# The first loads and transposes by halves, and the last chunks of the last half by quarters, in a two-layer encoder trunk

## The chip, the cores and the metric

The kernel runs on one NeuronCore of one Trainium2 chip, alone. The metric is the device time of one execution in microseconds, from start to end. It is given as the median of several executions.

## The reference, cut to what matters

Two layers of a post-norm encoder trunk over 256 tokens of width 1024: SwiGLU, a mixer, SwiGLU, each followed by a layer norm of the scaled residual. Layer 0 has a bidirectional mLSTM as its mixer, layer 1 a windowed attention. All data are float32.

```
D_MODEL = 1024; SEQ = 256; DEPTH = 2; D_FF = 2816; ALPHA = (2 * DEPTH) ** 0.25

def layer_norm(x, g, b):
    mu = mean(x, -1);  var = mean((x - mu) ** 2, -1)
    return (x - mu) * rsqrt(var + 1e-5) * g + b

def swiglu(x, w_in, w_out):
    gu = x @ w_in
    g, u = gu[..., :D_FF], gu[..., D_FF:]
    return (silu(g) * u) @ w_out

for l in range(DEPTH):
    x = layer_norm(ALPHA * x + 0.5 * swiglu(x, ffn_w_in[l, 0], ffn_w_out[l, 0]), ln_g[l, 0], ln_b[l, 0])
    x = layer_norm(ALPHA * x + mixer(x), ln_g[l, 1], ln_b[l, 1])     # mLSTM in layer 0, attention in layer 1
    x = layer_norm(ALPHA * x + 0.5 * swiglu(x, ffn_w_in[l, 1], ffn_w_out[l, 1]), ln_g[l, 2], ln_b[l, 2])
```

## The kernel before

**Split operands.** Every float32 operand of a product is held as two float32r tiles, a high part (a rounded copy, made by ScalarE for weights) and a low part (the difference, made by VectorE). One product is three matmuls: high by high, high by low, low by high (`mm3`). Nearly all matmuls have a 128x128 stationary operand and 512 columns of the moving one. In the profile the products with the input weights write banks named pw (`wbank`, four buffers), and the products with the output weights write banks named py (`ybank`, four buffers). The two pools share the eight banks of PSUM.

**Weights.** The class `Weights` holds a plan, a list of pieces of 128x1024 float32 in the order of their use. `load` starts the transfer of a piece on SyncE's queue (SP) as soon as a raw buffer is free; there are `RAW_BUFS = 4` buffers named w_raw for these. `high` makes w_hi on ScalarE, and `low` makes w_lo on VectorE and then gives the raw buffer back, so that `load` can start the next transfer. Piece 0 alone is split in two steps of 512 columns (the `if i == 0`). Which of these steps stands where in the engines' instruction streams is set by a model of the engines' times (`Paced`) during the feed-forward stages.

**The input.** x lies as two tiles of 128 tokens (x_69 and x_70 in the listings below, t = 0 and 1 in the code). Each is loaded in two halves of 512 columns on ScalarE's queue, between the first weight loads on SP: x0's first half, piece 0, x1's first half, piece 1, x0's second half, x1's second half, then the other pieces. `to_xT` transposes four blocks of 128x128 of one half on TensorE into a bank of its own and splits them into xT_hi and xT_lo. These banks are kept (`turned`), because four sums and differences of the transposed halves (S1 to S4) are made from them later.

**The start.** `ffn` is called first with `pending` of None. It puts out 14 transposes of the identity that nobody reads (`warm`), transposes the first half of x0, splits piece 0, and puts out 8 more idle transposes. `first_mm` then takes the products of pieces 0 and 1 in an order written out by hand: with a = 0 (piece 0, which holds the rows k = 0 and 1 of the reduction) the two products of high by high for x0, the transposes of x1's first half, then the other products of x0 and those of x1; with a = 1 first the transposes of both second halves.

**The end.** `tail` finishes a stage. For the last one it has six chunks c of the hidden layer left, for two token tiles t and two halves o of the output columns: y[t][o] is a bank of 128x512. Tile 0 goes first, both halves; each half is then added to the residual and its statistics are taken (`Norm.half`), and `Norm.finish` applies the layer norm. Tile 1 goes in the order half 1 with chunks 0 to 2, half 0 with all six, half 1 with chunks 3 to 5. After that VectorE does the last half, and `finish(1)`: aggregate the statistics, 1/sqrt by a power on GpSimd, subtract the mean and multiply by g in two halves, multiply by 1/sqrt and add b in two halves, and after each of the latter a DMA of that half of the result on SP. With `last`, `cuts` holds the two halves.

All instructions of the wrapped engines carry line 138 in the profile, since a helper records them.

Of the kernel before, what the change touches and what calls it, by code (L numbers as in the profile page):

```python
# [146 lines left out]
class Weights:  # L147
# [66 lines left out]
    def high(self):  # L214

        nc, i = self.nc, self.made
        p = self.plan[i]
        while self.half and (p["word"] not in self.raw or any(h[0] == p["needs"] for h in self.half)):
            self.low()
        while any(s_[0] == p["needs"] or p["word"] not in self.raw for s_ in self.sums):  # L220
            self.sum()
        if p["word"] not in self.raw:
            return False
        scale, raw = p["scale"], self.raw[p["word"]]
        hi = self.pool.tile([128, D], FR, name="w_hi", tag="w_hi", bufs=RING)
        if i == 0:
            for j in range(2):
                s_ = slice(j * 512, j * 512 + 512)
                nc.scalar.copy(hi[:, s_], raw[:, s_])
        elif scale is None:  # L230
            nc.scalar.copy(hi, raw)
        else:
            nc.scalar.activation(hi, raw, AF.Copy, scale=scale())
        self.half.append((i, hi))
        self.made += 1
        return True

    def low(self):

        nc = self.nc  # L240
        i, hi = self.half.pop(0)
        p = self.plan[i]
        k, scale, raw = p["k"], p["scale"], self.raw[p["word"]]
        lo = self.pool.tile([128, D], FR, name="w_lo", tag="w_lo", bufs=RING)
        if i == 0:
            for j in range(2):
                s_ = slice(j * 512, j * 512 + 512)
                nc.vector.tensor_sub(lo[:, s_], raw[:, s_], hi[:, s_].bitcast(F32))
        elif scale is None:
            nc.vector.tensor_sub(lo, raw, hi.bitcast(F32))  # L250
        else:
            nc.vector.scalar_tensor_tensor(lo, raw, scale(), hi.bitcast(F32), op0=OP.mult, op1=OP.subtract)
        self.parts[i] = (hi.rearrange("p (k f) -> p k f", k=k), lo.rearrange("p (k f) -> p k f", k=k))
        self.sums += [(i, *sum_) for sum_ in self.after.get(i, ())]
        self.drop(p["word"])
        self.load()
# [64 lines left out]
def trunk_kernel(ctx: ExitStack, tc: tile.TileContext, x, ffn_w_in, ffn_w_out, ln_g, ln_b, ml_w_in, ml_gate_b,  # L321
# [28 lines left out]
    def wide(w, r0, c0):  # L350
        piece(two(w, r0, c0), 2)
# [37 lines left out]
    for j, (kind, l, i, _) in enumerate(stages):  # L389
        if kind == "ffn":  # L390
            wi, wo = ffn_w_in[l, i], ffn_w_out[l, i]
            nth = iter(range(2 * UNITS))

            def down(n):
                for _ in range(n):
                    rows(wo, next(nth))

            for c0 in (0, F):
                for a in range(4):
                    wide(wi, a * 256, c0)  # L400
            for g in range(GROUPS):
                c0 = 512 + 768 * g
                for a in range(4):
                    beside(wi, a * 256, c0, F + c0)
                down(2)
                seven(wi, c0 + 256, F + c0 + 256, lambda i_: down(1) if g < GROUPS - 1 or i_ < 2 else None)
            down(6)
        elif kind == "mlstm":
            for c0 in (1024, 1536):
                for a in range(4):  # L410
                    wide(ml_w_in[0], a * 256, c0)
            for c0 in range(0, 1024, 256):
                for a in range(2):
                    narrow(ml_w_in[0], a * 512, c0)
            for c0 in (2048, 2560):
                for a in range(4):
                    wide(ml_w_in[0], a * 256, c0)
            for c in range(8):
                rows(ml_w_out[0], c, (lambda c=c: gcol[:, c:c + 1]))
        else:  # L420
            for c0 in (1024, 0):
                for a in range(4):
                    wide(at_w_in[0], a * 256, c0)
            for c0 in (512, 768):
                for a in range(2):
                    narrow(at_w_in[0], a * 512, c0)
            for c in range(8):
                rows(at_w_out[0], c)
        ends[j] = len(words)
# [98 lines left out]
    class Norm:  # L528
        def __init__(self, t, ca, eps, gb, last=False):
            self.t, self.ca, self.eps, self.gb, self.last = t, ca, eps, gb, last  # L530
            self.stats = state.tile([128, 2, 6], F32, name="stats", tag="stats", bufs=2)

        def half(self, h, y):
            z = xt[self.t][:, h * 512:(h + 1) * 512]
            nc.vector.scalar_tensor_tensor(z, z, self.ca, y, op0=OP.mult, op1=OP.add)
            nc.vector.bn_stats(self.stats[:, h], z)

        def finish(self, spare):
            mv = state.tile([128, 2], F32, name="mv", tag="mv", bufs=2)
            nc.vector.bn_aggr(mv, self.stats)  # L540
            rs = state.tile([128, 2], F32, name="rs", tag="rs", bufs=2)
            nc.vector.tensor_scalar(rs[:, 0:1], mv[:, 1:2], self.eps, None, op0=OP.add)
            nc.gpsimd.tensor_tensor(rs[:, 1:2], rs[:, 0:1], mhalf[:, 0:1], op=OP.pow)
            z = xt[self.t]
            cuts = [slice(0, 512), slice(512, D)] if self.last or self.t and LC[bound[0]] else [A]
            for s_ in cuts:
                nc.vector.scalar_tensor_tensor(z[:, s_], z[:, s_], mv[:, 0:1], self.gb[0][:, s_],
                                               op0=OP.subtract, op1=OP.mult)
            if len(cuts) == 1:
                W.done(0, spare)  # L550
            for s_ in cuts:
                nc.vector.scalar_tensor_tensor(z[:, s_], z[:, s_], rs[:, 1:2], self.gb[1][:, s_],
                                               op0=OP.mult, op1=OP.add)
                if self.last:
                    nc.sync.dma_start(out[0, tok(self.t), s_], z[:, s_])
            if len(cuts) > 1:
                W.done(0, spare)

    def tail(y, h, todo, first, norm, last, turn_at, between=None):

        def one(t, o, n):
            c, (i, w) = todo[t][n]
            mm3(y[t][o], h(c, t), pair(w, A, 0, slice(o * 512, o * 512 + 512)), first and n == 0, n == len(todo[t]) - 1)

        for o in range(2):
            for n in range(len(todo[0])):
                if between is not None and o == 1 and n == turn_at:
                    between()
                one(0, o, n)
            norm[0].half(o, y[0][o])  # L570
        norm[0].finish(0)
        full = len(todo[1])
        half = full // 2
        order = [(1, n) for n in range(half)] + [(0, n) for n in range(full)] + [(1, n) for n in range(half, full)]
        more = iter(RS[8 * bound[0]:8 * bound[0] + 8])
        for j, (o, n) in enumerate(order):
            if j == full + turn_at:
                emit_x(0, last)
            one(1, o, n)
            if j >= half and (n < half) == (o == 0):  # L580
                W.done(todo[1][n][1][0] + 1, next(more))
            if n == full - 1:
                norm[1].half(o, y[1][o])
        norm[1].finish(1)
        W.done(most=TD[bound[0]])
        return lambda: emit_x(1, last)
# [5 lines left out]
    def ffn(l, i, n, pending, last):  # L592
        with ExitStack() as ph:
# [10 lines left out]
            start = pending is None  # L604
            if start:
                warm(14)
                to_xT(0, xt[0], ybank, (0,), nc.vector.tensor_copy)
                W.split(1)
                warm(8)
            hs, pieces = [], []  # L610

            def tr(hB, t, h):
# [15 lines left out]

            def first_mm(ps, a):

                def mm(t, i, j):
                    for k in (2 * a, 2 * a + 1):
                        nc.tensor.matmul(ps[t], xT[i][:, k, tok(t)], pieces[a][j][:, k % 2], start=i == j == k == 0,
                                         stop=False)

                if a == 1:
                    for t in range(2):
                        to_xT(t, xt[t], ybank, (1,))
                pieces.extend(W.take(1))
                mm(0, 0, 0)  # L640
                if a == 0:
                    to_xT(1, xt[1], ybank, (0,))
                    W.split(2)
                mm(0, 1, 0)
                if a == 0:
                    mm(0, 0, 1)
                mm(1, 0, 0)
                if a == 0:
                    mm(1, 0, 1)
                mm(1, 1, 0)  # L650
                if a == 1:
                    mm(0, 0, 1)
                    mm(1, 0, 1)
# [757 lines left out]
```

## Time and profile before

| what | value |
|---|---|
| median of 3 executions | 930.31 us (929.8 to 930.38) |
| the profiled execution | 929.11 us |
| its span, from the first to the last instruction | 927.4 us |
| outside the span | 1.7 us |
| TensorE matmuls busy | 916.2 us (99% of the span) |
| VectorE busy | 784.6 us (85%) |
| ScalarE busy | 543.9 us (59%) |

The profile is of one execution. Times in it are microseconds from the first instruction. PE is TensorE, PEld its weight loads, DVE is VectorE, ACT is ScalarE, POOL is GpSimd, SP is SyncE; a q behind an engine's name is its queue, from which DMAs are issued. In the timeline a row gives start, duration, engine, line, operation, result and operands, form, and the number of like instructions; in brackets stands how long the engine had been idle before it, and what ended that. In the chain of waits a row gives start, duration and what the time was spent on. The granted clock of TensorE is a share of its full speed.

### The profile page before, as it was taken

What the parts mean: (1) busy time and instruction counts of PE and PEld (TensorE: products, weight loads), DVE (VectorE), ACT (ScalarE), POOL (GpSimd) and SP (SyncE); (2) the same over time, 40 slices, a digit from 0 to 9 for tenths busy, and PEclk for the clock granted to TensorE, in tenths of its full rate; (3) what the DMA queues carried; (4) which work ended last, traced back from release to release, by engine and by line L of the source; (5) the groups of instructions that cost most, each with busy time, mean ns of one, the idle gap of its engine ahead of it and who ended that gap; (6) DMA issues with size and microseconds to landing.
All of it is one profiled execution on the core that took longest, in us unless ns stands there. A gap on an engine that the chain in (4) does not pass through costs nothing.

```text
span 927.4 us, 12512 instructions
## 1 busy us (share of the span) xinstructions
PE 916.2 (99%) x4506; PEld 766.4 (83%) x4506; DVE 784.6 (85%) x948; ACT 543.9 (59%) x766; POOL 99.8 (11%) x144
## 2 busy tenths in 40 slices
PE   9999999999999999999999999999999999999996
PEld 7788888889988888888888888888888888888885
DVE  5899997886699799988887998978868878998875
ACT  5656756347564548565646666564568555757460
POOL 0010103011111010101010101010435300110100
PEclk9999999999999999999999999999999999999999
DMA  8979773646536949685558697737434385969421
GB/s 283 351 179 323 207 267 74 229 132 191 197 109 209 333 105 343 168 300 136 167 182 309 170 321 211 252 69 226 147 132 132 95 275 198 274 192 347 122 86 45
DMA packets 98461, 187.54 MB, mean 202 GB/s; under 512 B 6720, under 2 KB 37456, under 8 KB 98400
## 3 DMA queue, kind: packets, MB, share of 16 engines
q1 hardware_dynamic: 91072, 173.04, 54.4%
q0 software_dynamic: 6752, 12.66, 8.6%
q10 hardware_dynamic: 576, 1.05, 0.3%
q8 instruction: 35, 0.57, 0.2%
q14 instruction: 26, 0.21, 0.1%
HBM read 185.68 MB, written 1.05 MB: 201 GB/s over the span
## 4 chain that ended last, share of the span: by engine, by line
PE 91%; DVE 5%; ACT 2%; issue 1%; POOL 1%; DMA 0%; DVEq 0%; ACTq 0%; POOLq 0%
PE pw L138 58%; PE py L138 33%; DVE w_lo L138 2%; DVE h L138 1%; DMA w_raw<-in_ffn_w_in_dram 0%; ACT w_hi L138 0%; DVE wt L138 0%; POOL sc L1272 0%; DVE sc L138 0%; DVE a_lo L138 0%; DVE hst L138 0%; ACT S_hi L138 0%; DVE pr_lo L138 0%; ACT h L138 0%; DVE x L138 0%
## 5 line engine op out<-in xcount | busy, mean ns | idle before, releaser
L138 DVE TENSOR_TENSOR w_lo<-w_raw,w_hi 128x1024 fp32r<-128x1024 f32 (+1 forms) x237 | 281.8, 1219 | 25.9 <-ACT w_hi L138 23.8
L138 ACT CAST w_hi<-w_raw 128x1024 fp32r<-128x1024 f32 (+1 forms) x237 | 241.1, 1048 | 80.7 <-PE py L138 24.1
L138 PE MATMUL pw<-w_hi,xT_hi 128*128 128x512 f32 x560 | 221.8, 397 | 0.0
L138 PE MATMUL pw<-w_lo,xT_hi 128*128 128x512 f32 x560 | 217.5, 390 | 0.5 <-DVE w_lo L138 0.5
L138 PE MATMUL pw<-w_hi,xT_lo 128*128 128x512 f32 x560 | 218.0, 390 | 0.0
L138 ACT CAST w_hi<-s_raw 128x1024 fp32r<-128x1024 f32 x144 | 148.1, 1052 | 76.6 <-DVE s_raw L138 41.6
L138 DVE TENSOR_TENSOR w_lo<-s_raw,w_hi 128x1024 fp32r<-128x1024 f32 x144 | 172.8, 1219 | 21.2 <-ACT w_hi L138 20.5
L138 PE MATMUL py<-w_hi,h_hi 128*128 128x512 f32 x352 | 138.0, 392 | 0.0
L138 PE MATMUL py<-w_lo,h_hi 128*128 128x512 f32 x352 | 137.1, 390 | 0.0
L138 PE MATMUL py<-w_hi,h_lo 128*128 128x512 f32 x352 | 137.1, 389 | 0.0
L138 PEld LDWEIGHTS pw<-w_lo,xT_hi 128*128 128x128 f32 x560 | 105.3, 188 | 22.0 <-DVE w_lo L138 1.6
L138 PEld LDWEIGHTS pw<-w_hi,xT_lo 128*128 128x128 f32 x560 | 105.0, 188 | 22.4
L138 PEld LDWEIGHTS pw<-w_hi,xT_hi 128*128 128x128 f32 x560 | 105.1, 188 | 20.5 <-ACT w_hi L138 0.5
L138 DVE TENSOR_TENSOR s_raw<-s_raw 128x1024 f32<-128x1024 f32 x72 | 87.1, 1220 | 1.0
L267 POOL DMA_DIRECT2D s_raw<-in_ffn_w_in_dram x24 | 29.2, 1215 | 509.3 <-DVE w_lo L138 468.3
L138 PEld LDWEIGHTS py<-w_hi,h_lo 128*128 128x128 f32 x352 | 66.1, 188 | 13.9
L138 PEld LDWEIGHTS py<-w_lo,h_hi 128*128 128x128 f32 x352 | 66.1, 188 | 13.7 <-DVE w_lo L138 0.3
L138 PEld LDWEIGHTS py<-w_hi,h_hi 128*128 128x128 f32 x352 | 66.1, 188 | 13.4
L138 PE MATMUL pw<-w_hi,S_hi 128*128 128x512 f32 x192 | 74.7, 389 | 0.0
L138 PE MATMUL pw<-w_lo,S_hi 128*128 128x512 f32 x192 | 74.7, 389 | 0.0
L138 PE MATMUL pw<-w_hi,S_lo 128*128 128x512 f32 x192 | 74.7, 389 | 0.0
L138 DVE TENSOR_TENSOR h_lo<-pw,h_hi 128x512 fp32r<-128x512 f32 x44 | 30.1, 687 | 26.7 <-ACT h_hi L138 26.6
(206 smaller groups left out, 1087.2 us busy)
## 6 DMA issues: line engine op xcount, KB each, us to landing
w_raw<-in_ffn_w_out_dram SPq DMA_DIRECT2D x88, 512.0 KB, 5.1
s_raw<-in_ffn_w_in_dram SPq DMA_DIRECT2D x72, 512.0 KB, 6.1
w_raw<-in_ffn_w_in_dram SPq DMA_DIRECT2D x56, 512.0 KB, 5.1
w_raw<-in_ffn_w_in_dram SPq DMA_DIRECT2D x96, 256.0 KB, 4.3
s_raw<-in_ffn_w_in_dram POOLq DMA_DIRECT2D x24, 512.0 KB, 6.1
w_raw<-in_ml_w_in_dram SPq DMA_DIRECT2D x24, 512.0 KB, 4.6
w_raw<-in_at_w_in_dram SPq DMA_DIRECT2D x12, 512.0 KB, 4.2
w_raw<-in_ml_w_out_dram SPq DMA_DIRECT2D x8, 512.0 KB, 3.7
```

The costliest lines, as they stand in the source:

```text
L138: r = f(out, *args, **kw)
L267: nc.gpsimd.dma_start(t.rearrange("p (k f) -> p k f", k=self.words[w]["k"]), v, accum_op=OP.add)
```

## The change

Four edits, at the two ends of the program.

1. Piece 0 is loaded by two DMAs, one for each of its two blocks k of 512 columns, and piece 1 is split by halves as piece 0 is.
2. At the start the first two of the four transposes of x0's first half go to a bank of their own (`early`, a pw bank), and are split at once by VectorE alone. All four are then transposed again into the bank that is kept, of which the last two are split. The second group of idle transposes has 6 instead of 8.
3. In `first_mm` with a = 0, only the product with k = 0 stands ahead of the transposes of x1, and the product with k = 1 behind them.
4. At the end the accumulation of half 1 of tile 1 is closed after chunks 0 to 2 and added to the scaled residual (`first`). Chunks 3 to 5 go into two new pw banks of 128x256, one for each quarter; each quarter is added and its statistics are taken as it is done (`quarter`), so that there are three sets of statistics. The last scaling goes in pieces of 512, 256 and 256 columns, and the last of their three DMAs is issued from ScalarE's queue.

The diff:

```
 def high / def low:
-        if i == 0:
+        if i < 2:
             for j in range(2):
                 s_ = slice(j * 512, j * 512 + 512)
...
                 for a in range(4):
-                    wide(wi, a * 256, c0)
+                    if j == c0 == a == 0:
+                        piece([two(wi, 0, 0)[:, k:k + 1] for k in range(2)], 2)
+                    else:
+                        wide(wi, a * 256, c0)
...
     class Norm:
-            self.stats = state.tile([128, 2, 6], F32, name="stats", tag="stats", bufs=2)
+            self.stats = state.tile([128, 3, 6], F32, name="stats", tag="stats", bufs=2)
+            self.parts = 2
...
+        def first(self, h, y):
+
+            z = xt[self.t][:, h * 512:(h + 1) * 512]
+            nc.vector.scalar_tensor_tensor(z, z, self.ca, y, op0=OP.mult, op1=OP.add)
+
+        def quarter(self, h, q, y):
+            z = xt[self.t][:, h * 512 + q * 256:h * 512 + (q + 1) * 256]
+            nc.vector.tensor_add(z, z, y)
+            nc.vector.bn_stats(self.stats[:, h + q], z)
+            self.parts = 3
...
-            nc.vector.bn_aggr(mv, self.stats)
+            nc.vector.bn_aggr(mv, self.stats[:, 0:self.parts])
...
-            for s_ in cuts:
+            if self.parts == 3:
+                cuts = [slice(0, 512), slice(512, 768), slice(768, D)]
+            for n_, s_ in enumerate(cuts):
...
-                    nc.sync.dma_start(out[0, tok(self.t), s_], z[:, s_])
+                    (nc.scalar if n_ == 2 else nc.sync).dma_start(out[0, tok(self.t), s_], z[:, s_])
...
     def tail:
-            mm3(y[t][o], h(c, t), pair(w, A, 0, slice(o * 512, o * 512 + 512)), first and n == 0, n == len(todo[t]) - 1)
+            end = n == len(todo[t]) - 1 or last and t == o == 1 and n == len(todo[t]) // 2 - 1
+            mm3(y[t][o], h(c, t), pair(w, A, 0, slice(o * 512, o * 512 + 512)), first and n == 0, end)
...
+            if last and j == full + half:
+                break
             one(1, o, n)
+            if last and j == half - 1:
+                norm[1].first(1, y[1][1])
...
+        if last:
+            for q in range(2):
+                yq = wbank((128, 256))
+                for n in range(half, full):
+                    c, (i, w) = todo[1][n]
+                    mm3(yq, h(c, 1), pair(w, A, 0, slice(512 + 256 * q, 768 + 256 * q)), n == half, n == full - 1)
+                norm[1].quarter(1, q, yq)
...
     def ffn:
                 warm(14)
-                to_xT(0, xt[0], ybank, (0,), nc.vector.tensor_copy)
+                early = wbank((128, 2, 128))
+                for k in range(2):
+                    nc.tensor.transpose(early[:, k], xt[0][:, tok(k)], ident)
+                split_evac(pair(xT, A, slice(0, 2), tok(0)), early, high=nc.vector.tensor_copy)
+                late = ybank((128, 4, 128))
+                for k in range(4):
+                    nc.tensor.transpose(late[:, k], xt[0][:, tok(k)], ident)
+                turned[0, 0] = late
                 W.split(1)
-                warm(8)
+                split_evac(pair(xT, A, slice(2, 4), tok(0)), late[:, 2:4])
+                warm(6)
...
     def first_mm:
-                def mm(t, i, j):
-                    for k in (2 * a, 2 * a + 1):
+                def mm(t, i, j, ks=(2 * a, 2 * a + 1)):
+                    for k in ks:
...
-                mm(0, 0, 0)
                 if a == 0:
+                    mm(0, 0, 0, (0,))
                     to_xT(1, xt[1], ybank, (0,))
                     W.split(2)
-                mm(0, 1, 0)
+                    mm(0, 1, 0, (0,))
+                    mm(0, 0, 0, (1,))
+                    mm(0, 1, 0, (1,))
+                else:
+                    mm(0, 0, 0)
+                    mm(0, 1, 0)
```

What TensorE has in its stream at the start, before the change (x_69 and x_70 are the two token tiles, ident the identity; rows 1 and 3 are the idle transposes):

```order
1 L138 MATMUL py<-ident 128x128 x14
2 L138 MATMUL py<-ident,x_69 128x128 x4
3 L138 MATMUL py<-ident 128x128 x8
4 L138 MATMUL pw<-w_hi,xT_hi 128x512 x2
5 L138 MATMUL py<-ident,x_70 128x128 x4
6 L138 MATMUL pw<-w_hi,xT_lo 128x512 x2
7 L138 MATMUL pw<-w_lo,xT_hi 128x512 x2
8 L138 MATMUL pw<-w_hi,xT_hi 128x512 x2
9 L138 MATMUL pw<-w_lo,xT_hi 128x512 x2
10 L138 MATMUL pw<-w_hi,xT_lo 128x512 x2
11 L138 MATMUL py<-ident,x_69 128x128 x4
12 L138 MATMUL py<-ident,x_70 128x128 x4
```

And with the change, at the same place:

```order
1 L138 MATMUL py<-ident 128x128 x14
2 L138 MATMUL pw<-ident,x_69 128x128 x2
3 L138 MATMUL py<-ident,x_69 128x128 x4
4 L138 MATMUL py<-ident 128x128 x6
5 L138 MATMUL pw<-w_hi,xT_hi 128x512
6 L138 MATMUL py<-ident,x_70 128x128 x4
7 L138 MATMUL pw<-w_hi,xT_lo 128x512
8 L138 MATMUL pw<-w_hi,xT_hi 128x512
9 L138 MATMUL pw<-w_hi,xT_lo 128x512
10 L138 MATMUL pw<-w_lo,xT_hi 128x512 x2
11 L138 MATMUL pw<-w_hi,xT_hi 128x512 x2
12 L138 MATMUL pw<-w_lo,xT_hi 128x512 x2
```

The number of transposes ahead of the first product is 26 in both. One product of high by high has moved behind the transposes of x_70, so that ten matmuls stand between those and the next transposes before, and eleven now (rows 7 to 12 and two of w_hi by xT_lo).

VectorE's stream at the end of the program, from the last instructions of tile 0 (x_69) to the last of tile 1 (x_70), before:

```order
734 L138 SCALAR_TENSOR_TENSOR x_69<-x_69,rs,ln_b 128x512 x2
735 L138 SCALAR_TENSOR_TENSOR x_70<-x_70,py 128x512
736 L138 BN_STATS stats<-x_70 128x6
737 L138 SCALAR_TENSOR_TENSOR x_70<-x_70,py 128x512
738 L138 BN_STATS stats<-x_70 128x6
739 L138 BN_AGGR mv<-stats 128x2
740 L138 TENSOR_SCALAR rs<-mv 128x1
741 L138 SCALAR_TENSOR_TENSOR x_70<-x_70,mv,ln_g 128x512 x2
742 L138 SCALAR_TENSOR_TENSOR x_70<-x_70,rs,ln_b 128x512 x2
```

And now:

```order
735 L138 SCALAR_TENSOR_TENSOR x_69<-x_69,rs,ln_b 128x512 x2
736 L138 SCALAR_TENSOR_TENSOR x_70<-x_70,py 128x512 x2
737 L138 BN_STATS stats<-x_70 128x6
738 L138 TENSOR_TENSOR x_70<-x_70,pw 128x256
739 L138 BN_STATS stats<-x_70 128x6
740 L138 TENSOR_TENSOR x_70<-x_70,pw 128x256
741 L138 BN_STATS stats<-x_70 128x6
742 L138 BN_AGGR mv<-stats 128x2
743 L138 TENSOR_SCALAR rs<-mv 128x1
744 L138 SCALAR_TENSOR_TENSOR x_70<-x_70,mv,ln_g 128x512 x2
745 L138 SCALAR_TENSOR_TENSOR x_70<-x_70,rs,ln_b 128x512
746 L138 SCALAR_TENSOR_TENSOR x_70<-x_70,rs,ln_b 128x256 x2
```

The residual of the last half is now scaled ahead of the first half's (row 736 holds both), two pairs of an addition and its statistics over 256 columns stand where one pair over 512 stood, and the last scaling has three steps instead of two. Between the two places the streams of all engines hold the same instructions in the same order.

More of the change, by code (lines that the diff above doesn't have):

```diff
@@ L244, in low @@
         lo = self.pool.tile([128, D], FR, name="w_lo", tag="w_lo", bufs=RING)
-        if i == 0:
+        if i < 2:
             for j in range(2):
```

## The prediction

> **What bounds the kernel now.** First the page: the engines' busy times and the chain of work that ended last.
>
> ```profile
> PE 916.2 (99%) x4506; PEld 766.4 (83%) x4506; DVE 784.6 (85%) x948; ACT 543.9 (59%) x766; POOL 99.8 (11%) x144
> PE 91%; DVE 5%; ACT 2%; issue 1%; POOL 1%; DMA 0%; DVEq 0%; ACTq 0%; POOLq 0%
> ```
>
> TensorE (PE) holds 91% of the chain. The change leaves the middle of the program as it is, so only the pieces at the ends that aren't PE can go. Second, the chain of waits over the first 36 us, to see what the start hangs on:
>
> ```profile
> 1.45 4.63 PE py L138 x26
> 9.80 0.45 PE py L138 x4
> 10.28 1.07 ACT xT_hi L138 x2
> 11.36 0.96 ACT w_hi L138
> 12.34 1.24 DVE w_lo L138
> 13.59 4.55 DMA w_raw<-in_ffn_w_in_dram
> 18.16 1.06 ACT w_hi L138
> 19.25 1.23 DVE w_lo L138
> 32.31 1.15 DVE w_lo L138
> 33.50 2.56 PE pw L138 x10
> ```
>
> Read backwards: PE at 33.50 waits for a w_lo, and from 19.25 to there VectorE (DVE) and ScalarE (ACT) work one after the other. Before that a weight DMA takes from 13.59 to 18.14, which could start only when the w_lo of 12.34 gave its raw buffer back; that one hangs on the ACT steps of 10.28, and these on the transposes of x's second halves. So a microsecond saved before 9.64, where these begin, comes through to 33.50; one saved between 10 and 33 on PE alone does not. Third, the timelines of the first 10 us, and the landings of x's first two parts:
>
> ```profile
> 1.45 3.25 PE L138 MATMUL py<-ident 128*128 128x128 f32 x14 [1.45 <-DVE ident L138]
> 4.49 0.71 PE L138 MATMUL py<-ident,x 128*128 128x128 f32 x4
> 5.04 1.04 PE L138 MATMUL py<-ident 128*128 128x128 f32 x8
> 5.24 0.69 DVE L138 CAST xT_hi<-py 128x512 fp32r<-128x512 f32 x1 [3.85 <-PE py L138]
> 5.31 1.14 ACT L138 CAST w_hi<-w_raw 128x512 fp32r<-128x512 f32 x2 [1.03 <-DMA w_raw<-in_ffn_w_in_dram]
> 6.05 0.19 PEld L138 LDWEIGHTS pw<-w_hi,xT_hi 128*128 128x128 f32 x1 [0.21 <-ACT w_hi L138]
> 6.84 0.60 PE L138 MATMUL py<-ident,x 128*128 128x128 f32 x4
> 7.91 0.19 PEld L138 LDWEIGHTS pw<-w_lo,xT_hi 128*128 128x128 f32 x1 [0.21 <-DVE w_lo L138]
> 8.59 1.06 ACT L138 CAST w_hi<-w_raw 128x1024 fp32r<-128x1024 f32 x1 [0.52 <-DMA w_raw<-in_ffn_w_in_dram]
> 9.64 0.60 PE L138 MATMUL py<-ident,x 128*128 128x128 f32 x4
> x<-in_x_dram ACTq DMA_DIRECT2D x1, 256.0 KB, 3.6
> x<-in_x_dram ACTq DMA_DIRECT2D x1, 256.0 KB, 5.4
> ```
>
> The first part was issued at 0.8 and lands at 4.4; the second was issued at 1.2 and lands at 6.6, and x1's transposes stand at 6.84 (their weight load is 0.2 earlier). Fourth, the last 10 us on DVE, with the last matmuls, the power on GpSimd and the last DMAs:
>
> ```profile
> 917.70 0.39 PE L138 MATMUL py<-w_hi,h_hi 128*128 128x512 f32 x1
> 919.52 0.39 PE L138 MATMUL py<-w_hi,h_lo 128*128 128x512 f32 x1
> 917.90 0.69 DVE L138 SCALAR_TENSOR_TENSOR x<-x,py 128x512 f32<-128x512 f32 x1 [1.65 <-PE py L138]
> 918.62 0.70 DVE L138 BATCH_NORM_STATS2 stats<-x 128x6 f32<-128x512 f32 x1
> 919.94 0.69 DVE L138 SCALAR_TENSOR_TENSOR x<-x,py 128x512 f32<-128x512 f32 x1 [0.62 <-PE py L138]
> 920.67 0.69 DVE L138 BATCH_NORM_STATS2 stats<-x 128x6 f32<-128x512 f32 x1
> 921.39 0.21 DVE L138 BATCH_NORM_AGGREGATE mv<-stats 128x2 f32<-128x12 f32 x1
> 921.71 1.40 DVE L138 SCALAR_TENSOR_TENSOR x<-x,mv,ln_g 128x512 f32<-128x512 f32 x2
> 921.94 0.92 POOL L543 TENSOR_TENSOR rs<-rs,mhalf 128x1 f32<-128x1 f32 x1 [7.24 <-DVE rs L138]
> 923.03 1.41 DVE L138 SCALAR_TENSOR_TENSOR x<-x,rs,ln_b 128x512 f32<-128x512 f32 x2
> out_dram<-x SPq DMA_DIRECT2D x2, 256.0 KB, 2.0
> ```
>
> After the last matmul (ends 919.91) nothing hides anything: 1.5 us of adding and statistics, 3.1 us of normalising, and the last DMA, 2.0 us to landing.
>
> **The change part by part: the end.** PE: nine matmuls of 512 become eighteen of 256. The nine start 0.227 apart ((919.52 - 917.70) / 8), 2.04 us in all. The price of a 256-wide one comes from a stretch that is nearly all of these, and those of 256-wide DVE steps from the groups:
>
> ```profile
> 213.00:236.00 23.00, 23.00 (x195) 1.00 0.77 242
> L138 DVE TENSOR_TENSOR hh<-sg,pw 128x256 f32<-128x256 f32 x24 | 8.9, 414 | 0.0
> L138 DVE BATCH_NORM_STATS2 hst<-h 128x6 f32<-128x256 f32 x8 | 3.0, 414 | 0.0
> ```
>
> 23.00 / 195 is 0.118; with 0.12 the eighteen take 2.16, so PE ends 0.12 later. The first quarter is done at 917.70 + 9 x 0.12 + 0.17 (the 0.39 of a matmul less its pitch), about 918.95; the second at about 920.03. DVE: the scaling of the last half (`first`) can start when chunks 0 to 2 are done, 18 matmuls before 917.70, so about 913.7; it falls into DVE's idle 1.65 us before 917.90, takes 0.69 of it and costs nothing. Without that cover it would push back all that follows by 0.69. DVE ends the first half's statistics at 919.32. Then come four steps of 0.414, 1.66, with the 0.03 that lies between dependent steps: the aggregate starts near 921.05 instead of 921.39. PE's second quarter (920.03) is in time for its addition (about 920.2), so PE's 0.12 is hidden by DVE. Two of the steps don't depend on the one before, and two such steps of 512 overlap by about 0.08 (1.41 for two that take about 0.74 each): at best a gain of 0.47, at worst, if the aggregate over three sets takes 0.06 longer, 0.25. I take **-0.35**. The normalising keeps its 3.1 us: GpSimd ends at 922.86, 0.17 before DVE needs it, and both move together. The last scaling in three steps takes 0.74 + 2 x 0.41 less two overlaps of 0.08, 1.41 as before: nothing, at worst +0.1.
>
> The last DMA carries 128 KB instead of 256, from a queue where nothing is ahead of it (ACT has no work left; on SP the second piece goes out while DVE does the third). Two bounds: at the best rate that the trace shows,
>
> ```profile
> 4.00:5.00 1.00, 1.00 (x8) 1.00 1.05 404
> ```
>
> 404 GB/s, 128 KB are 0.32 us less. On the other side, a DMA from ACT's queue is seen only at the start, with 3.6 us to landing (256 KB, together with weights), 1.5 more than SP's 2.0. The nearest row is SP's store, in the same direction and place, so I take **-0.2**, with -0.35 to +0.1 for the range and the rest as a rival. The Trainium skill (Trainium Kernel Development and Optimization, Key Constraints) says that DMAs issued by SP, ACT and GpSimd share the same 16 DMA engines, and that issuing from several engines only saves the issue time of the sequencer. By that the choice of ACT's queue would bring nothing by itself, and the term would be the halved bytes alone, near -0.3; no run here shows a store from ACT yet.
>
> **The start.** PE has 26 transposes ahead of its first product in both versions. The first product waits 0.21 for w_hi now; with half of piece 0 landing between 4.4 (with x0) and 5.3 (as the whole does now), its copy of 0.57 is done by 5.0 to 5.9. DVE's two steps of about 0.41 on the early bank, from about 5.0, are done by 5.9. So the first product comes near 5.9, and after one product instead of two PE stands before x1's transposes near 6.1. There it waits for x1's first part, 6.6 now. Behind the transposes stand eleven matmuls instead of ten (+0.23), and the wait of 0.21 for w_lo at 7.91 goes, since both halves of w_lo are then done before PE needs them. If x1's part still lands at 6.6, the second halves' transposes come at 9.64 + 0.02, and with PE's other small gaps closed or not, -0.05 to +0.1. If it lands earlier, all of that comes earlier, up to 0.55: then ACT's own work stops it, since piece 1 lands at 8.57 and its copy in two halves takes 1.14, to 9.73, where the step now at 10.28 follows. Will it land earlier? Until the whole of piece 0 is in, x1's part shares the DMA engines with it, and after that with piece 1; its bytes and theirs are the same in both versions. But x1's part needed 2.2 us after x0's, in which 404 GB/s would carry 0.9 MB, against 0.26 MB of its own: a fair share with piece 0's second half alone would end near 5.7. I take half of the 0.55, **-0.25**, with +0.1 and -0.55 as ends. The extra steps of 256 and 512 on DVE and ACT cost about 0.3 us before 9 us, where both have waits (1.03 and 0.52 on ACT, above). SP has one more issue ahead of piece 1, whose data wait behind piece 0's anyway; and the issue of the fourth piece now waits for x0's landing at 4.4. Behind it on SP stand only loads that wait for the first raw buffer until about 7.9, so both cost nothing; without that cover a later issue would cost its own delay.
>
> **Sum.** -0.25 - 0.35 - 0.2 = -0.8: the profiled execution (span 927.4 and 1.7 outside it, 929.11) would be 928.3. It lies 1.2 below the median of 930.31, to which the same sum gives **929.5**.
>
> **The rivals.** *The start gives nothing*: x1's part lands at 6.6 as now. For it: the bytes in front of it are the same. Against: it shared with two transfers, and half of piece 0 comes free earlier. Sum -0.5: 929.8. The Trainium skill (DMA: Bandwidth & Descriptors, Queues, rings and completion order) says that each DMA engine takes turns between the queues packet by packet; by that, cutting a transfer of SP's queue in two changes nothing for ACT's queue, which is this rival. *The store from ACT's queue is late*: at the price of the 3.6, +1.5 in place of -0.2, sum +0.9: 931.2, slower than before. It decides from a landing of 2.6 us on, where the other 0.6 are used up. For it only the load at the start, which shared the engines; against it SP's stores at 2.0. *The clock falls*: the first 14 idle transposes start 0.22 apart and the eight behind 5.04 at most 0.13 (1.04 / 8), so PE goes at a higher rate from near 4.7 on. With the new pause before x1's transposes (6.1 to 6.6) it could fall back: all PE work up to 9.64, about 3.0 us, would take twice as long, +3.0 - 0.55 at the end, 932.8. It decides if the matmuls behind 6.6 start more than 0.3 apart. Against it: pauses of 0.2 now do nothing, and the granted clock is 1.00 in both window rows above. *More comes free*: ACT waits 1.42 for the DMA of the chain:
>
> ```profile
> 18.16 1.05 ACT L138 CAST w_hi<-w_raw 128x1024 fp32r<-128x1024 f32 x1 [1.42 <-DMA w_raw<-in_ffn_w_in_dram]
> ```
>
> If this DMA, issued earlier, met other traffic and took that much less, 928.1 at best.
>
> **How the numbers follow.** Forecast 0.50, the start gives nothing 0.33, late store 0.08, clock 0.03, more 0.06. All good ends give -0.55 - 0.47 - 0.35, about -1.4 (928.9), all bad ones +0.1 - 0.25 + 0.1 + 0.1, about +0.05 (930.4); the runs before spread over 0.6, so 0.3 to 0.4 more on each side: 928.5 to 930.7. About 0.2%, 1.86 us, is what a measurement of this kernel can tell from no change; forecast, first rival and nearly all of the late store stay within: 0.91. Faster is the last rival, 0.06; slower the clock, 0.03.
>
> **What would show it.** Right: x1's first transposes before 6.5, the second halves' before 9.5, the wait at 33.50 ending earlier by the same amount; the aggregate 1.1 us after PE's end instead of 1.5; the last landing under 2.0 us. Wrong: x1's transposes still at 6.8, the DVE steps of 256 over 0.45, the last store over 2.3, or a new wait of PE in the middle.

## The result, and the profile after

| kernel | median | runs |
|---|---|---|
| before, beside it | 929.80 us | 5, from 929.63 to 930.38 |
| after | 940.52 us | 5, from 939.78 to 941.66 |

The ratio is 1.0117, 95% interval 1.0106 to 1.0128: 10.7 us slower, where 929.5 was predicted. The profiled execution of after took 941.66 us, span 939.9. Beside each experiment below stands the kernel before on the same chip. Medians there are of 4 runs (stats_only, pad_128, pad_192) or of 10 or 11; phases and pairs were run once. One of the 11 runs of start_only took 3035.66 us and is left out of its ratio.

First the page of after, the engines' busy times:

```profile
PE 928.2 (99%) x4515; PEld 768.3 (82%) x4515; DVE 786.8 (84%) x954; ACT 544.1 (58%) x768; POOL 100.3 (11%) x144
```

PE is still busy for 99% of the span, and 12 us longer (916.2 before) with nine matmuls more, those of the quarters. So TensorE's own instructions have become dearer; no new wait of this size holds it up. Which ones, the groups by shape tell (busy us, mean ns of one), of before:

```profile
L138 PE MATMUL pw<-w_hi,xT_lo 128*128 128x512 f32 x560 | 218.0, 390 | 0.0
L138 PE MATMUL py<-w_hi,h_hi 128*128 128x512 f32 x352 | 138.0, 392 | 0.0
L138 PE MATMUL pw<-w_hi,S_hi 128*128 128x512 f32 x192 | 74.7, 389 | 0.0
```

and of after:

```profile
L138 PE MATMUL pw<-w_hi,xT_lo 128*128 128x512 f32 x560 | 218.5, 391 | 0.0
L138 PE MATMUL py<-w_hi,h_hi 128*128 128x512 f32 x349 | 139.0, 398 | 0.3 <-DVE S L138 0.3
L138 PE MATMUL pw<-w_hi,S_hi 128*128 128x512 f32 x192 | 75.9, 396 | 0.0
```

Matmuls whose stationary operand is h or S take 6 to 7 ns longer, those with xT don't. A mean hides where this is, so next the chain of waits (start, length, what), at pieces that are alike in both kernels. Before:

```profile
104.60 5.44 PE pw L138 x24
197.16 46.59 PE pw L138 x318
330.62 5.44 PE py L138 x24
653.03 9.52 PE pw L138 x42
742.16 9.52 PE pw L138 x42
```

After:

```profile
106.62 5.60 PE pw L138 x24
200.87 46.57 PE pw L138 x318
334.34 5.60 PE py L138 x24
662.26 9.54 PE pw L138 x42
751.37 9.54 PE pw L138 x42
```

The pieces of 24 are products of S alone (the pw one) and of h alone (the py one): 5.44 / 24 is a pitch (start to start) of 226.7 ns, 5.60 / 24 is 233.3. The pieces of 42 are products of xT, 226.7 before and 227.1 after (9.54 / 42), and the first mixer's piece of 318 doesn't change either. The starts lie apart by 2.0 us at 105, where the first stage is under way, by 3.7 at 197 and still 3.7 at 331, where the first mixer begins and where it is over, and by 9.2 at 653 and still 9.2 at 742, on both sides of the second mixer. So each feed-forward stage loses about 2.8 us and the mixers lose nothing; the first stage has lost 0.9 more, with its start (below). Four stages have 4 x 408 = 1632 such matmuls, 1623 of 512 columns in after: x 6.6 ns is 10.7 us, the whole loss.

The start of after, in PE's timeline:

```profile
5.15 0.69 PE L138 MATMUL pw<-ident,x 128*128 128x128 f32 x2 [0.46 <-DMA x<-in_x_dram]
6.49 1.34 PE L138 MATMUL py<-ident 128*128 128x128 f32 x6
10.88 1.03 PE L138 MATMUL py<-ident,x 128*128 128x128 f32 x8
```

and the transfers of x0's and x1's first parts (us from issue to landing, 3.6 and 5.4 before):

```profile
x<-in_x_dram ACTq DMA_DIRECT2D x1, 256.0 KB, 4.3
x<-in_x_dram ACTq DMA_DIRECT2D x1, 256.0 KB, 5.1
```

x1's part lands 0.3 earlier than before, as hoped, but x0's 0.7 later. That the change delays x0's part isn't shown: in the nine profiles of kernels without the new start it landed anywhere from 4.35 to 5.42 (5.11 here). PE pauses for it and then runs its idle transposes at 0.22 apiece instead of 0.13, and the second halves' transposes stand at 10.88 instead of 9.64. The end of after, in the timeline PE's last matmul and DVE's steps:

```profile
932.09 0.28 PE L138 MATMUL pw<-w_hi,h_lo 128*128 128x256 f32 x1
930.29 0.69 DVE L138 SCALAR_TENSOR_TENSOR x<-x,py 128x512 f32<-128x512 f32 x1 [1.21 <-PE py L138]
933.33 0.24 DVE L138 BATCH_NORM_AGGREGATE mv<-stats 128x2 f32<-128x18 f32 x1
934.99 1.54 DVE L138 SCALAR_TENSOR_TENSOR x<-x,rs,ln_b 128x512 f32<-128x512 f32 x3
```

and two of the last three stores, again with us to landing:

```profile
out_dram<-x SPq DMA_DIRECT2D x1, 256.0 KB, 2.0
out_dram<-x ACTq DMA_DIRECT2D x1, 128.0 KB, 2.0
```

From the addition of the first half to the aggregate it is 3.04 us now (933.33 - 930.29), 3.49 before (921.39 - 917.90). The store of half the bytes takes as long as the whole one.

### The profile page after: what moved, and what is told of

Same layout as the page of the kernel before. It is cut to its first block, busy times and chain, and to the rows that moved or that the text cites. A ratio compares the mean times of both kernels' runs of the same rounds, so it can differ in the third digit from the quotient of the medians.

```text
span 939.9 us, 12541 instructions
## 1 busy us (share of the span) xinstructions
PE 928.2 (99%) x4515; PEld 768.3 (82%) x4515; DVE 786.8 (84%) x954; ACT 544.1 (58%) x768; POOL 100.3 (11%) x144
## 4 chain that ended last, share of the span: by engine, by line
PE 86%; DVE 8%; ACT 2%; DMA 2%; issue 1%; POOL 1%; DVEq 0%; ACTq 0%; POOLq 0%
PE pw L138 55%; PE py L138 31%; DVE w_lo L138 3%; ACT w_hi L138 1%; DMA w_raw<-in_ffn_w_out_dram 1%; DVE h L138 1%; ACT S_hi L138 0%; DVE S L138 0%; DMA x<-in_x_dram 0%; DMA w_raw<-in_ffn_w_in_dram 0%; DVE s_raw L138 0%; DVE x L138 0%; DVE wt L138 0%; POOL sc L1314 0%; DVE sc L138 0%
```

## The experiments

**Theory A.** No instruction of the middle was edited, but one line reaches there: the tile `stats` grew from 2 x 6 to 3 x 6 numbers. Tiles are rounded up to 32 bytes, so each of its two buffers takes 96 bytes of a partition instead of 64, and everything allocated behind it lies 64 bytes further on: mean, rate and all tiles of the stages, h and S among them. x, xT and the weights are allocated ahead of it and stay:

```
              before    after    distance from w_hi, modulo 256: before, after
w_hi          34912     34912
xT_hi         125024    125024   0    0
h_hi          141664    141728   0    64
S1_hi         170336    170400   0    64
```

Theory A says that the distance between the stationary and the moving tile in a partition sets the pitch. **Theory B**, the rival: the places do nothing, and the slower matmuls come from what else the change did, the banks that rotate differently, the transfers shifted by one, the order.

**stats_only** and **after_packed** tell these apart: the one line without the rest, and the rest without the one line's effect.

```diff
 # stats_only, from before
-            self.stats = state.tile([128, 2, 6], F32, name="stats", tag="stats", bufs=2)
+            self.stats = state.tile([128, 3, 6], F32, name="stats", tag="stats", bufs=2)
...
-            nc.vector.bn_aggr(mv, self.stats)
+            nc.vector.bn_aggr(mv, self.stats[:, 0:2])
 # after_packed, from after
-            mv = state.tile([128, 2], F32, name="mv", tag="mv", bufs=2)
+            mr = state.tile([128, 4], F32, name="mr", tag="mr", bufs=2)
+            mv, rs = mr[:, 0:2], mr[:, 2:4]
...
-            rs = state.tile([128, 2], F32, name="rs", tag="rs", bufs=2)
```

> The kernel before with one edit: the tile of the statistics has three places of six numbers instead of two, and only two are used, so that every tile allocated behind it lies 64 bytes further on in each partition and nothing else changes. Theory A (where the stationary h and S tiles lie against the weights sets the pitch of their matmuls): the 512-wide matmuls of h and S go from 227 to 233 or 234 ns in all four FFN stages, about 10.6 us in all, so 940 to 941 us. Theory B (the loss comes from the changed order, the banks or the transfers, and the places of the tiles are without effect): 229.8 +- 0.3 on top of 700, that is 929.5 to 930.1 us, pitch 227 ns.

> The kernel after with the mean, the variance and the two numbers of the rate in one tile of 16 bytes instead of two of 8, so that this tile with the larger statistics takes as much room as all three took before and the stage's tiles lie exactly where the kernel before has them; the order, the banks and the transfers are those of the kernel after. Theory A: the pitch of the h and S matmuls is back at 227 ns and what is left are the two edits themselves, start +0.5 and end -0.5 to 0: 929.5 to 930.5 us. Theory B: nothing comes back, 940 to 941 us.

stats_only: 939.42 us against 929.22, ratio 1.0113 (1.0097 to 1.0128). after_packed: 929.35 against 929.22, ratio 1.0002 (0.9993 to 1.0012). One piece of S products in the chain of each, stats_only first:

```profile
105.29 5.60 PE pw L138 x24
```

```profile
105.07 5.44 PE pw L138 x24
```

The one line makes the whole loss, and the whole loss goes when the tiles are put back. Theory B falls.

**pad_128, pad_192, pad_256** shift the stage's tiles in the kernel before by an unused tile (128, 192 or 256 bytes), with no other edit. **pad_all_64** puts one of 64 bytes ahead of the weights, so that all tiles move together.

```diff
 # pad_128, behind xT; 48 and 64 numbers for pad_192 and pad_256
+    pad = state.tile([128, 32], F32, name="pad", tag="pad")
+    nc.gpsimd.memset(pad, 0.0)
 # pad_all_64, behind neg_id among the constants
+    pad = consts.tile([128, 16], F32, name="pad")
+    nc.gpsimd.memset(pad, 0.0)
```

> The kernel before with an unused tile of 128 bytes ahead of the statistics, so that all stage tiles lie 128 bytes further on. Theory A with a period of 128 bytes or less (only the place within 128 bytes counts): 929.5 to 930.3 us, pitch 227 ns. Theory A with a longer period (only the old distance, or a multiple of 256 and more, is good): 940 us or another loss, pitch over 230 ns. Theory B: 929.5 to 930.3 us.

> The kernel before with an unused tile of 256 bytes ahead of the statistics: h and S lie 256 bytes further on. Theory A with a period of 256 bytes: 929 to 930 us and pitch 227 ns. Theory A with no period (only the old distance is good) : 939 to 941 us.

> The kernel before with an unused tile of 64 bytes among the constants, ahead of the weights, so that x, xT, the weights, h and S all lie 64 bytes further on and keep their distances. Theory A as a matter of distance between the stationary and the moving tile: 929.5 to 930.3 us, pitch 227 ns everywhere. Theory A as a matter of the absolute place of the stationary tile: h and S lose as in the kernel after, and xT's matmuls, 227 ns so far, lose as well: 945 us or more. Theory B: 929.5 to 930.3 us.

> The kernel before with an unused tile of 192 bytes ahead of the statistics. TensorE alone gave 228.8 ns at a distance of 192 bytes against 226.7 at 0. Theory A with the numbers of TensorE alone: 1632 matmuls of h and S in the four FFN stages, 2.1 ns each, 3.4 us: 932.6 to 933.2 us. If in the kernel every distance but 0 costs the same: 939 to 941 us.

| kernel | distance mod 256 | median, before beside it | ratio, interval |
|---|---|---|---|
| pad_128 | 128 | 939.26, 929.22 | 1.0104 (1.0089 to 1.0119) |
| pad_192 | 192 | 933.41, 929.60 | 1.0043 (1.0030 to 1.0057) |
| pad_256 | 0 | 929.29, 929.50 | 0.9999 (0.9990 to 1.0008) |
| pad_all_64 | 0 | 929.35, 929.22 | 1.0001 (0.9991 to 1.0011) |

So it is the distance and not the place, and it repeats at 256 bytes: 64 and 128 cost 10 us, 192 costs 3.8, 256 nothing. For pad_192 the expectation was worked out from TensorE alone (next experiment), 3.4 us; a piece of 24 in its chain has 5.49 / 24 = 228.8 ns:

```profile
105.28 5.49 PE pw L138 x24
```

**phases** measures the pitch by itself, with all other engines silent: 16 stationary tiles (sa to sp) at distances of 0, 32, ... 480 bytes (results ra to rp), then one stationary tile with the moving slice shifted (ma to mp), then the first row 256 wide (na to np).

```diff
+    def group(o, s, m0, width, n):
+        for i in range(n):
...
+            r = slice(m0 + (i % 2) * width, m0 + (i % 2) * width + width)
+            nc.tensor.matmul(o, hi, w_hi[:, r], start=i == 0, stop=False)
+            nc.tensor.matmul(o, hi, w_lo[:, r], start=False, stop=False)
+            nc.tensor.matmul(o, lo, w_hi[:, r], start=False, stop=i == n - 1)
```

> Leaves the whole computation out: TensorE alone, three matmuls per chunk as in the kernel (high by high, high by low, low by high), 48 in a row for each case. First 512 wide with 16 stationary tiles, each 32 bytes further from the moving tile than the one before (0 to 480 bytes, modulo 512); then one stationary tile and the moving slice shifted by 32 bytes at a time; then the first row again 256 wide. Theory A with a period of 256 bytes: a mean near 390 ns (pitch 227) at distances of 0 and 256, 395 to 396 ns (pitch 232 to 234) at 64 and 128 and their like, in both rows, whichever of the two tiles is moved. Theory A with another period: the short mean comes at 0 only (512 bytes) or at more places. Whether any distance gives less than 227 is open. If the pitch does not depend on the distance here, the loss in the kernel needs the other engines' traffic as well.

Its chain of waits is one piece of 48 matmuls per case:

```profile
24.10 10.89 PE ra L138 x48
34.99 11.19 PE rb L138 x48
46.18 11.20 PE rc L138 x48
...
68.62 11.16 PE re L138 x48
...
90.98 10.99 PE rg L138 x48
...
113.17 10.89 PE ri L138 x48
...
224.32 11.00 PE mc L138 x48
...
380.47 5.74 PE na L138 x48
...
397.55 5.63 PE nd L138 x48
```

Divided by 48, the lengths give pitches of 226.9 ns at 0 and again at 256 (ri), 233.3 at 64, 232.5 at 128, 229.0 at 192, 233 to 234 at the odd multiples of 32 (rb, and the three left out). Moving the other tile mirrors it (mc is -64, that is 192, and has 229.2). The period is 256 bytes and no other engine is needed. 226.9 is the least: the kernel before had the best distance, for h, S and xT alike. One product had not, that of q with the output weights in the second mixer, at 128 in before, and it bears the rule out in the kernels: the 32 matmuls py<-w_lo,q_hi start 232 ns apart in before, 229.5 in after (now at 192), 232.8 in pad_192 (at 64) and 227.5 in pad_128 (at 0). 256 wide the order turns round, but by little: 119.6 at 0, 117.3 at 96.

**pairs** asks which stationary tile counts for a matmul's pitch, its own or the one that is loaded for the next while it streams.

```diff
+    run("pa", [(a, 0)])
+    run("pc", [(c, 0)])
+    run("pac", [(a, 0), (c, 0)])
+    run("paacc", [(a, 0), (a, 0), (c, 0), (c, 0)])
+    o = run("pm", [(a, 0), (a, 0), (a, 8), (a, 8)])
```

> Leaves the whole computation out: TensorE alone, 48 matmuls 512 wide in a row per case against one moving slice, with a stationary tile at distance 0 (sa) and one at distance 64 bytes (sc): first sa alone, sc alone, the two in turn, then two of the one and two of the other in turn; at last sa alone with the moving slice in turn twice at 0 and twice 32 bytes on. Theory N (what counts is the stationary tile that is being loaded for the next matmul while the moving one streams): alone 227 and 233 ns as before; in turn, the matmul of sa has the long pitch, since sc is loaded under it, and that of sc the short one; in twos, both have one long and one short, mean 230 for each. Theory O (a matmul's own stationary tile counts): in turn and in twos sa 227, sc 233. In the last case both theories give the long pitch to the matmuls of the shifted slice, 227 and 233 in twos.

Its chain, 48 matmuls per case:

```profile
23.66 10.88 PE pa L138 x48
34.54 11.20 PE pc L138 x48
45.74 11.05 PE pac L138 x48
56.78 11.12 PE paacc L138 x48
67.90 11.13 PE pm L138 x48
```

Alone 226.7 and 233.3; in turn 230.2, between the two; in twos 231.7. In turn, the starts put 228.5 on the matmuls of sa and 231.5 on those of sc on the mean; in twos, 231.4 and 232.1 (without the first two of each tile), and the last case has 231.9 where both theories wanted 230. Theory N wanted 233 and 227, and 230 for both; theory O 227 and 233 both times. Neither holds. The single starts in the trace show why such means say little: in turn the distances from one start to the next go round by four, 226, 236, 231 and 227 ns (after sa, sc, sa, sc), though the tiles repeat by two, and with sc alone they alternate between 236 and 231. So a pitch doesn't belong to a pair of neighbours alone, and by what mechanism the distance acts stays open. The Trainium skill (SBUF — State Buffer, Who interferes with whom) gives PE two independent read ports, one for the moving operand and one for the weight load, and lets only a port pair of other engines cause contention. That table doesn't speak of addresses; taken as it stands, the distance would cost nothing. The measured 227 to 233 ns decide against this, without showing that it is these two reads that meet.

**start_only** and **end_only** size the change's own two edits, each alone in the kernel before with all tiles at their old places (end_only with the packed tile of after_packed); their diffs are the parts of the change's diff.

> The kernel before with the edits of the start alone, all tiles at their places. Theory A leaves here only what the start does itself: transposes of x1 and h1 0.1 to 0.3 us earlier, but weights that land no earlier, since the transfers between 23 and 47 us follow each other without a gap; so the wait of 0.9 us at 33.5 us goes and waits of about 1.3 us near 60 us come: 0 to +0.5 us, 929.2 to 929.8 us. By the prediction on record -0.25 us, 929.0 us.

> The kernel before with the edits of the end alone (three chunks by quarters, three scalings and stores), the stage's tiles kept at their places by putting mean, variance and rate into one tile. The end as predicted (sum of its terms -0.4 us) less the store term, which the kernel after showed to be nothing (2.03 us for 128 KB): -0.5 to 0 us against before, 928.8 to 929.3 us. If the tail's three steps cost more than the aggregate gains: +0.2 us or more.

start_only: 929.98 against 929.50, ratio 1.0006 (0.9997 to 1.0015). end_only: 930.41 against 929.50, ratio 1.0010 (1.0001 to 1.0019). Neither brings a gain. start_only can't be told from before; end_only is 0.9 us slower, with an interval just clear of 1, and 1.1 us above the upper end of what was expected. The start in the trace of start_only, PE:

```profile
9.92 1.03 PE L138 MATMUL py<-ident,x 128*128 128x128 f32 x8
33.12 0.50 PE L138 MATMUL pw<-w_lo,xT_hi 128*128 128x512 f32 x1
62.30 0.50 PE L138 MATMUL py<-w_lo,h_hi 128*128 128x512 f32 x1 [0.23 <-DVE w_lo L138]
```

and the same two places in before:

```profile
33.50 0.50 PE L138 MATMUL pw<-w_lo,xT_hi 128*128 128x512 f32 x1 [0.55 <-DVE w_lo L138]
62.31 0.50 PE L138 MATMUL py<-w_lo,h_hi 128*128 128x512 f32 x1
```

The matmul that waited at 33.50 comes 0.38 earlier without a wait, though the second halves' transposes stand 0.28 later here than before (9.92 and 9.64). At 62.30 the gain is gone: there PE waits for the next w_lo, which is no earlier. after_packed waits there as well (62.78). So whatever is gained before 62 us, nothing of it comes through. The end in end_only's trace, with the start of the same trace:

```profile
5.47 1.11 PE L138 MATMUL py<-ident,x 128*128 128x128 f32 x4 [0.77 <-DMA x<-in_x_dram]
6.38 1.91 PE L138 MATMUL py<-ident 128*128 128x128 f32 x8
919.37 0.69 DVE L138 SCALAR_TENSOR_TENSOR x<-x,py 128x512 f32<-128x512 f32 x1 [1.03 <-PE py L138]
922.44 0.24 DVE L138 BATCH_NORM_AGGREGATE mr<-stats 128x2 f32<-128x18 f32 x1
```

First half to aggregate: 3.07 us, 0.42 less than before. From the first half to the last landing it is 8.32 (927.69 - 919.37), 8.60 before (926.50 - 917.90): of the 0.42 the last scaling in three steps takes 0.12 back (1.53 for 1.41). That this execution as a whole isn't shorter lies at its start, where nothing was edited: x0's first part landed 1.1 us later than in before's profile, PE paused, and its eight idle transposes took 1.91 us instead of 1.04. Whether all of end_only's runs had that, and so whether it explains the 0.9 us, is open.

**warm_18** and **best** tried to use this: four more idle transposes, so that PE doesn't pause before x0's landing, and with them the end by quarters, without its third scaling and store.

```diff
 # both
-                warm(14)
+                warm(18)
 # best, from end_only
-            if self.parts == 3:
-                cuts = [slice(0, 512), slice(512, 768), slice(768, D)]
...
```

> The kernel before with 18 idle transposes at its start instead of 14, so that TensorE does not stand still before x's first part lands (which came between 4.35 and 5.42 us in the profiles so far). Theory S (the spread of a microsecond and more between runs comes from the start, where a pause of TensorE before that landing can put off the rise of its rate): the slow draws go, the runs lie closer together, 928.5 to 929.3 us, median 0.2 to 0.6 us under before. Rival: the four transposes cost their own 0.4 to 0.8 us where x's part lands early, and the rate is not governed by that pause: 929.5 to 930.3 us.

> The kernel before with the three chunks of the end by quarters, all tiles at their old places, the last scaling and store in two parts as before, and 18 idle transposes at the start. The end gave 0.42 us at the aggregate in two traces and its third scaling took 0.12 back, so without that part 0.4 us remain: 0.4 us under the kernel with 18 idle transposes alone, that is 928.2 to 929.1 us by theory S, 929.1 to 929.9 by its rival.

warm_18: 929.67 against 929.60, ratio 1.0001 (0.9992 to 1.0010), and its runs spread over 2.1 us (928.97 to 931.09) where before's 21 spread over 2.9. Theory S fell: neither the median nor, clearly, the spread got better. Two traces speak against its mechanism too, that a pause of PE puts off the rise of its rate; the eight idle transposes in pad_all_64, where PE didn't pause for x0's part, and in pad_256, where it did:

```profile
5.42 1.91 PE L138 MATMUL py<-ident 128*128 128x128 f32 x8
```

```profile
5.35 0.83 PE L138 MATMUL py<-ident,x 128*128 128x128 f32 x4 [0.56 <-DMA x<-in_x_dram]
6.01 1.04 PE L138 MATMUL py<-ident 128*128 128x128 f32 x8
```

They took 1.91 us without a pause and 1.04 behind one of 0.56. What sets the time of the rise stays open.

best: 929.35 against 929.60, ratio 0.9996 (0.9987 to 1.0005); in its trace the last landing comes 8.21 us after the first half is added (926.74 - 918.53), 0.39 less than before. That is what the quarters gain, and it is smaller than what separates two runs: best can't be told from before.

## Why the prediction was wrong

- **The failed step** is this: "The change leaves the middle of the program as it is, so only the pieces at the ends that aren't PE can go." The instructions of the middle stayed, their operands' places did not. The growth of `stats` by 24 bytes a buffer stood in the diff and got no term in the sum, which puts it at nothing without a reason; stats_only puts 10.2 us on it, through the pitch of the h and S matmuls, 233.3 ns instead of 226.7. None of the rivals had it, and the sign of "a new wait of PE in the middle", which was to show the prediction wrong, would have missed it too: the loss is in the pitch, not in waits.
- **The start, -0.25.** Of its two conditions the first held in part: x1's part landed 5.1 us after its issue instead of 5.4, and x1's transposes and the second halves' stood at 6.57 and 9.54 in after_packed (6.84 and 9.64 before), just short of the 6.5 and 9.5 that were to show it right. In after they stood at 7.91 and 10.88, since x0's part came at 5.1 and PE ran its transposes at the lower rate. The second condition failed: the chain to 33.50 was followed, but not what lies behind it. The wait there hid the next one at 62.3, so the size was 0, the first rival's number, though not by its reason, by which cutting piece 0 changes nothing for x1's part: that part landed between 6.2 and 6.4 in the three profiles with the cut (after, after_packed, start_only) and between 6.4 and 7.5 in the nine others without it. So the Trainium skill's rule (DMA: Bandwidth & Descriptors, Queues, rings and completion order), as the prediction drew on it, isn't borne out here. It isn't refuted either: the same edit moves the issue of SP's fourth piece from 2.31 to 5.13, and no run tells the two apart.
- **More comes free**, the last rival, met its condition: the weight DMA that took 4.55 us in the chain of before took 3.69 in after_packed and 3.83 in after (first and second line), and 3.89 in start_only. That, and not an earlier start, is what freed the wait at 33.50 in start_only. It brought nothing, since at 62 us PE waited again; and in end_only, whose start is unchanged, such a DMA took 3.66 as well (issued at 16.03), so the cut isn't shown to be its cause.

```profile
13.48 3.69 DMA w_raw<-in_ffn_w_in_dram
14.82 3.83 DMA w_raw<-in_ffn_w_in_dram
```

- **The clock falls**, the third rival, had no chance to show itself: x1's part was there before PE was (6.2 and 6.57 in after_packed), so the pause that it needs didn't come up, and the eleven matmuls behind x1's transposes went at 0.23 apiece (2.53 / 11).
- **The aggregate, -0.35**: -0.45 in after and -0.42 in after_packed and end_only. Right in mechanism and nearly in size; it comes 0.96 us after PE's end (933.33 less 932.37), where 1.1 was forecast.
- **PE's +0.12 hidden**: the 18 quarter matmuls go at 0.118, and the aggregate came early all the same. Right.
- **The last scaling in three steps, 0, at worst +0.1**: 1.54 instead of 1.41. Slightly beyond its worst end.
- **The last store, -0.2**: 128 KB took 2.03 us to landing from ACT's queue and 2.05 from SP's, 256 KB 2.04 in before. The term is 0. The transfer's bytes hardly count at this size, and the estimate from 404 GB/s was wrong by its whole 0.3. The rival of a late store on ACT's queue did not come true either.

The end by itself makes -0.28 us at the last landing (end_only, after_packed) where -0.55 was forecast, the start makes nothing, and the two together no measured difference (after_packed). All of the result is the term that was not on the list.

## What to carry to other kernels

Before a change to a kernel bound by TensorE is costed, look at the addresses of its operands in both builds: a tile that grows by a few bytes moves all that is allocated behind it. A loss that builds up evenly over the stages, with PE busy and no new waits, points to a change of the matmuls' pitch; compare pieces of the same matmuls in the two chains before looking for waits. And follow a saved wait on to the next one that ends at the same time, or its size is only a bound.

## What the runs showed of the hardware

- The pitch of float32r matmuls 512 wide depends on the distance in SBUF between the stationary and the moving tile, modulo 256 bytes: 226.9 ns at 0, 229 at 192, 232 to 234 elsewhere in steps of 32. 256 wide it is 119.6 at 0 and 117.3 to 119.8 elsewhere.
- It acts with TensorE alone at work (phases), and moving both tiles by 64 bytes changed nothing (pad_all_64).
- The rise of TensorE's rate in the first microseconds doesn't need an unbroken row of matmuls: eight idle transposes took 1.91 us without a pause before them (pad_all_64) and 1.04 behind one of 0.56 us (pad_256).
- A last store of 128 KB lands as late as one of 256 KB, 2.03 and 2.04 us after its issue.
